# Half of the NSA output projection set between the last attention units of a hybrid decoder layer

## The chip, the core and the metric

The kernel runs on one core of a Trainium2 chip. The core has a matrix engine (TensorE, PE in the profile; its weight loads are listed as PEld), two elementwise engines that can read the accumulation banks (VectorE, DVE, and ScalarE, ACT), a third one, GpSimd (POOL), and SyncE (SP), which issues DMAs. Each engine works through its own queue in order and waits for the others by semaphores. The metric is the device time of one execution in microseconds (us); less is better.

## The reference, cut to what matters

```python
y_mla = mla_mixer(...)                    # 8 heads, causal softmax, width 512
y_nsa = nsa_mixer(...)                    # 8 heads in 2 groups, three gated branches, width 512
mixed = concatenate([rmsnorm(y_mla, g_out_mla), rmsnorm(y_nsa, g_out_nsa)], -1)
h = x + mixed @ w_o                       # (512, 1024) @ (1024, 1024)
a = relu(rmsnorm(h, g_mlp_norm) @ w_up)   # 1024 -> 4096
h = h + (a * a) @ w_down                  # 4096 -> 1024
out = rmsnorm(h, g_final)
```

There are 512 tokens, which the kernel treats as four tiles of 128 (t = 0 to 3), and everything is float32. Since `mixed` is two halves of 512 columns, `mixed @ w_o` is a sum of two products: an MLA part, and an NSA part that needs `y_nsa` of the same tokens.

## The kernel before

**Precision.** A float32 product is made of three passes on PE: each operand is split into a rounded high half and a low half (`split`, line 117: the high half by an ACT cast on line 111, the low half by a DVE subtraction on line 125), and `mm3` (lines 130 to 132) multiplies high by high, high by low and low by high.

**Attention.** Twenty-four units run one behind another in a software pipeline: eight MLA heads (s = 0 to 7), eight NSA units of the selected branch (s = 8 to 15), and eight NSA units that do the window and the compressed branch (s = 16 to 23: tokens t = 0, 1, 2, 3, two groups each). A unit writes scores into bank "A" (`s_ps`, lines 547 and 548), DVE masks them and takes the maximum (lines 552 and 556), ACT takes the exponential (line 560), PE transposes (`pt_ps`, line 585), ACT and DVE split, PE multiplies by the values (`ot_ps`, lines 596 and 597), ACT copies the result (`os`, line 619), PE folds it (`o_ps`, lines 621 and 623), DVE weighs it (`ow`, line 626) and POOL adds it into `yn` (line 629). A unit takes three rounds, so those of t = 0 are complete when s = 20 begins, those of t = 1 when s = 22 begins.

**Filling.** Between the steps of the units `fill(s)` takes steps of other work from two lanes. The second lane is `out_mla`: it loads and splits the MLA half of `w_o` and does the eight MLA products of the output projection (`out_proj`, lines 809 to 818: 12 matrix products of 128x512 into `wo_ps`, then one DVE addition into `xs` on line 818). The last of the eight (t = 3, columns 512 to 1023) is held back (`HELD`), until s is at least 22 (`FROM`). Right after it `load_wo` loads and splits the last quarter of `w_o` (the NSA half, columns 512 to 1023), on POOL (lines 798, 115 and 125).

**After the units.** `norm_y` squares and sums `yn` of all four tiles (ACT, line 783; `rsq` on DVE and POOL), `transpose_y` turns each tile on PE (`yt_ps`, line 805) and splits it into `yth` and `ytl`. The pools of the attention are released, so that the loads of `w_up` (`ur`, line 950, on the SP queue) can start. Then, for two column halves c and four tiles t, comes the NSA product of the projection (`out_proj(1, t, c, ...)` in bank "A", which has two buffers), the transposition of the sum (`ht_ps`, line 1080, bank "B"), a DVE scaling into `hs` (line 1082), and in between the splits that the MLP begins with: three tiles of `w_up` (`uw`), and token tiles `ttB11`, `ttT2`, `ttT1`, `ttB21` of which T2 needs all of `hs` for c = 0 and a DVE subtraction (line 1089) stands ahead of T1. The first MLP products (`up_ps`, line 990) use B11 (48 passes), then T2 (48), then B21.

**Order.** The queues are not in the order of the source: a scheduler places each engine's instructions when the program is built, so the diff doesn't tell where the work ends up.

Of the kernel before, what the change touches and what calls it, by code (L numbers as in the profile page):

```python
# [20 lines left out]
NT = T // P  # L21
# [5 lines left out]
RATES = (1.2, 1.2, 1.2, 1.0, 0.5, 1.4)  # L27
# [1 line left out]
ORDER = ((1, 2, 3, 0), (0, 1, 2, 3))  # L29
LAG = (0, 0)  # L30
CMPF = 0
HELD = 1
FROM = 22
SLACK = 8
WARM = 36
CSUM = "V"
QTE = "AAAA"
# [57 lines left out]
def layer(ctx, tc, x, xt, w_in, w_uq, w_ukv, w1k, w2k, w1v, w2v, w_o, w_up, w_down, g_final, consts, vecs, out):  # L95
    nc = tc.nc
# [74 lines left out]
    m = {}  # L171
# [39 lines left out]
    def steps(*gens):  # L211
        for g in gens:
            yield from g
# [562 lines left out]
    ny, ry = col(40, 8), col(48, 8)  # L776
    sh, r4 = col(56, 8), col(64)

    def norm_y(y, part):
        for t in range(NT):  # L780
            jy = m["wo"].tile([P, 4, P], F32, tag="wor", name="jy", bufs=2).rearrange("p a b -> p (a b)")
            at = 4 * part + t
            nc.scalar.activation(jy, y[:, t], AF.Square, accum_out=ny[:, at:at + 1])
            rsqrt_mean(ry[:, at:at + 1], ny[:, at:at + 1], 512)
# [37 lines left out]
    def out_mla():  # L822

        m["yth"] = m["wo"].tile([P, 4, 512], R32, name="yth")
        m["ytl"] = m["wo"].tile([P, 4, 512], R32, name="ytl")
        w = [load_wo(0, V_OM, 0, *WO_[0])]
        yield
        norm_y(ym, 0)
        yield
        for t in range(NT):  # L830
            sync.dma_start(m["xs"][:, t, :], x_t[:, t, :])
        for t in range(NT):
            transpose_y(ym, t, m["yth"][:, t], m["ytl"][:, t], "F")
            yield
        w.append(load_wo(0, V_OM, 1, *WO_[1]))
        todo = [(t, c) for c in range(2) for t in range(NT)]
        for n, (t, c) in enumerate(todo):
            if n == len(todo) - HELD:
                m["held"] = True
                yield  # L840
            yield from out_proj(0, t, c, w[c], m["yth"][:, t], m["ytl"][:, t], "F", 1)
            yield
            if (t, c) == (NT - 1, 0):
                m["won"] = [load_wo(1, V_ON, 0, *WO_[2])]
        m["won"].append(load_wo(1, V_ON, 1, *WO_[3]))

# [4 lines left out]
    lanes = [[(0, 6, RATES[0], chunk(C_CMP, "wc", post_c)), (0, 7, RATES[1], chunk(C_Q[0], "wq", post_q(0))),  # L853
              (0, 9, RATES[2], chunk(C_Q[1], "wq", post_q(1))), (6, 9, RATES[3], turn_q(0)), (10, 10, 1.0, turn_q(1)),
              *([] if CMPF else [(10, 17, RATES[4], steps(compressed(0), compressed(1)))])],
             [*([(10, 17, RATES[4], steps(compressed(0), compressed(1)))] if CMPF else []), (10, len(units) + 2, RATES[5], out_mla())]]
    due = [0.0, 0.0]
    live = []

    marks = []  # L860

    def fill(s):
        marks.append(next(i for i in reversed(nc.cur_bb.bb.instructions) if i.engine == mybir.EngineType.PE))
        for n, fills in enumerate(lanes):
            if fills and s >= fills[0][0]:
                due[n] += fills[0][2]
                while due[n] >= 1.0 and fills and s >= fills[0][0]:
                    due[n] -= 1.0
                    if n == 1 and m.get("held"):
                        if s < FROM:  # L870
                            break
                        with tc.issue_after(marks[-1 - SLACK]):
                            r = next(fills[0][3], "done")
                    else:
                        r = next(fills[0][3], "done")
                    if r == "done":
                        fills.pop(0)

    for s in range(len(units) + 2):
# [26 lines left out]
        for f in fills:  # L906
            whole(f[3])

    norm_y(yn, 1)
    w, yth, ytl = (m[n] for n in ("won", "yth", "ytl"))  # L910
    for t in range(NT):
        transpose_y(yn, t, yth[:, t], ytl[:, t], "B")
    wk2.release()
    wk.release()
# [157 lines left out]
    ready = []  # L1072
    for c in range(2):
        for t in range(NT):
            whole(out_proj(1, t, c, w[c], yth[:, t], ytl[:, t], "A"))
            cs = slice(512 * c, 512 * c + 512)
            b = bank("B", "ht_ps")
            for j in range(4):
# [181 lines left out]
```

## Time and profile before

| | |
|---|---|
| time, median of 3 runs | 652.48 us (652.03 to 653.15) |
| the profiled execution | 652.88 us, of which the span from first to last instruction is 651.0 us |
| PE busy | 635.2 us, 98% of the span |
| DVE, ACT, POOL busy | 429.9, 336.6, 240.0 us |
| clock of TensorE granted | 0.997 of full speed |

The stage that the change touches runs from 223 us (the first scores of the window units) over 276.9 us (the last matrix product of the attention) to 308.7 us (the first MLP product with T2). "Busy" of PE counts a modelled tail of each matrix product, so that neighbours overlap; the distance between two starts is the time that one costs.

### The profile page before, as it was taken

What the parts mean: (1) busy time and instruction counts of PE and PEld (TensorE: products, weight loads), DVE (VectorE), ACT (ScalarE), POOL (GpSimd) and SP (SyncE); (2) the same over time, 40 slices, a digit from 0 to 9 for tenths busy, and PEclk for the clock granted to TensorE, in tenths of its full rate; (3) what the DMA queues carried; (4) which work ended last, traced back from release to release, by engine and by line L of the source; (5) the groups of instructions that cost most, each with busy time, mean ns of one, the idle gap of its engine ahead of it and who ended that gap; (6) DMA issues with size and microseconds to landing.
All of it is one profiled execution on the core that took longest, in us unless ns stands there. A gap on an engine that the chain in (4) does not pass through costs nothing.

```text
span 651.0 us, 10981 instructions
## 1 busy us (share of the span) xinstructions
PE 635.2 (98%) x4092; PEld 571.5 (88%) x4092; DVE 429.9 (66%) x898; ACT 336.6 (52%) x702; POOL 240.0 (37%) x294
## 2 busy tenths in 40 slices
PE   7999999999999999999999999999999999999996
PEld 5989999998878888889998889988899988999885
DVE  5767577856788589768967435794259843497425
ACT  5567677857946478732884115541144521355213
POOL 3864402235783139613110225413154231344031
PEclk9999999999999999999999999999999999999998
DMA  6533210105322101063135313254122541124003
GB/s 193 154 99 82 68 50 17 33 2 195 99 78 88 33 2 33 1 216 108 46 116 163 98 33 98 88 171 131 33 81 63 181 140 55 63 68 147 15 2 129
DMA packets 47125, 56.53 MB, mean 87 GB/s; under 512 B 4320, under 2 KB 34784, under 8 KB 47072
## 3 DMA queue, kind: packets, MB, share of 16 engines
q1 hardware_dynamic: 46784, 55.57, 27.9%
q8 instruction: 32, 0.52, 0.3%
q10 hardware_dynamic: 288, 0.26, 0.1%
q14 instruction: 21, 0.17, 0.1%
HBM read 53.72 MB, written 2.10 MB: 86 GB/s over the span
## 4 chain that ended last, share of the span: by engine, by line
PE 86%; DVE 5%; DMA 3%; ACT 2%; POOL 2%; issue 1%; SPq 1%; POOLq 0%; ACTq 0%; DVEq 0%
PE up_ps L990 25%; PE dn_ps L131 9%; PE dn_ps L132 9%; PE dn_ps L130 9%; PE wo_ps L130 2%; PE wo_ps L132 2%; PE wo_ps L131 2%; PE pt_ps L585 2%; PE hid_ps L730 2%; PE s_ps L547 1%; PE pt_ps L692 1%; PE ot_ps L596 1%; PE wq_ps L132 1%; PE wq_ps L131 1%; PE wq_ps L130 1%; PE s_ps L548 1%
## 5 line engine op out<-in xcount | busy, mean ns | idle before, releaser
L130 PE MATMUL dn_ps<-dw,ah 128*128 128x512 f32 (+1 forms) x264 | 101.9, 386 | 0.0
L131 PE MATMUL dn_ps<-dw,ah 128*128 128x512 f32 (+1 forms) x264 | 101.9, 386 | 0.0
L132 PE MATMUL dn_ps<-dw,al 128*128 128x512 f32 (+1 forms) x264 | 101.7, 386 | 0.0
L990 PE MATMUL up_ps<-ttT,uw 128*128 128x256 f32 x720 | 89.5, 282 | 0.4
L990 PEld LDWEIGHTS up_ps<-ttT,uw 128*128 128x128 f32 x720 | 87.2, 189 | 1.0 <-ACT snap L1019 1.0
L990 PE MATMUL up_ps<-ttB,uw 128*128 128x256 f32 x648 | 82.0, 282 | 0.0
L990 PEld LDWEIGHTS up_ps<-ttB,uw 128*128 128x128 f32 x648 | 79.6, 189 | 0.5
L958 POOL TENSOR_TENSOR us<-us,ur 128x1024 f32<-128x1024 f32 x14 | 41.4, 2958 | 101.2 <-DVE uw L125 101.2
L958 POOL TENSOR_TENSOR us<-ur 128x1024 f32<-128x1024 f32 x14 | 35.3, 2530 | 99.8 <-DMA ur<-in_w_up 49.7
L125 DVE TENSOR_TENSOR uw<-us,uw 128x1024 fp32r<-128x1024 f32 x28 | 37.4, 1336 | 47.2 <-ACT uw L111 47.2
L125 DVE TENSOR_TENSOR dw<-dr,dw 128x1024 fp32r<-128x1024 f32 x32 | 43.8, 1368 | 35.3 <-ACT dw L111 35.3
L131 PEld LDWEIGHTS dn_ps<-dw,ah 128*128 128x128 f32 x264 | 49.6, 188 | 10.6
L130 PEld LDWEIGHTS dn_ps<-dw,ah 128*128 128x128 f32 x264 | 49.6, 188 | 10.5
L132 PEld LDWEIGHTS dn_ps<-dw,al 128*128 128x128 f32 x264 | 49.5, 188 | 10.6
L111 ACT CAST uw<-us 128x1024 fp32r<-128x1024 f32 x28 | 29.4, 1049 | 55.5 <-PE dn_ps L132 40.7
L125 DVE TENSOR_TENSOR uw<-ur,uw 128x1024 fp32r<-128x1024 f32 x25 | 39.5, 1582 | 25.6 <-ACT uw L111 25.6
L111 ACT CAST dw<-dr 128x1024 fp32r<-128x1024 f32 x32 | 33.2, 1048 | 38.0 <-PE dn_ps L132 21.5
L111 ACT CAST uw<-ur 128x1024 fp32r<-128x1024 f32 x25 | 26.2, 1049 | 29.9 <-PE dn_ps L132 26.7
L560 ACT ACTIVATE pr<-pr,mx 128x256 f32<-128x256 f32 (+3 forms) x64 | 36.0, 565 | 6.9 <-DVE mx L552 5.2
L125 DVE TENSOR_TENSOR pl<-pt_ps,ph 128x512 fp32r<-128x512 f32 (+3 forms) x60 | 34.2, 577 | 8.2 <-ACT ph L111 6.9
L111 ACT CAST ph<-pt_ps 128x512 fp32r<-128x512 f32 (+3 forms) x60 | 29.7, 499 | 15.5 <-PE pt_ps L585 5.4
L1156 DVE SCALAR_TENSOR_TENSOR xs<-dn_ps,small,xs 128x512 f32<-128x512 f32 (+1 forms) x33 | 23.0, 734 | 19.9 <-PE dn_ps L132 19.9
(326 smaller groups left out, 1533.5 us busy)
## 6 DMA issues: line engine op xcount, KB each, us to landing
ur<-in_w_up SPq DMA_DIRECT2D x32, 512.0 KB, 3.9
dr<-in_w_down SPq DMA_DIRECT2D x32, 512.0 KB, 3.8
wor<-in_w_o SPq DMA_DIRECT2D x16, 256.0 KB, 3.1
wqraw<-in_w_in SPq DMA_DIRECT2D x16, 128.0 KB, 2.2
xs<-in_x SPq DMA_DIRECT2D x4, 512.0 KB, 5.4
wmraw<-in_w_in SPq DMA_DIRECT2D x8, 208.0 KB, 4.3
xr<-in_xt SPq DMA_DIRECT2D x3, 512.0 KB, 3.8
out<-xs SPq DMA_DIRECT2D x6, 256.0 KB, 2.2
```

The source lines that it names most:

```text
L111: nc.scalar.copy(dst, src)
L125: (lo_eng or nc.vector).tensor_tensor(lo, src, hi.bitcast(F32), op=ALU.subtract)
L130: nc.tensor.matmul(o, a_hi, b_hi, start=first, stop=False)
L131: nc.tensor.matmul(o, a_hi, b_lo, start=False, stop=False)
L132: nc.tensor.matmul(o, a_lo, b_hi, start=False, stop=last)
L547: nc.tensor.matmul(S[:, :b - a], qs, ka[:, brg, a:b], start=True, stop=False)
L560: nc.scalar.activation(pr[:, :L], pr[:, :L], AF.Exp, bias=lim, scale=-1.0, accum_out=sums[:, 4 + h:5 + h])
L585: nc.tensor.transpose(b[:, h * P:(h + 1) * P], prs[h][:, j * P:(j + 1) * P], ident)
L730: nc.tensor.matmul(hp[0:96, 0:P], xx[:, 2 * i:2 * i + 16 * 95 + 1:16], w1[:, j, :], start=(i == 0), stop=(i == 15))
L958: add = lambda o, x, y: nc.gpsimd.tensor_tensor(o, x, y, op=ALU.add)
L990: nc.tensor.matmul(oj, v[:, x, k, s], t[:, y, k, :], start=first and j == 0 and k == 0 and n == 0, stop=k == 3 and n == 2, skip_group_chec ...
L1156: nc.vector.scalar_tensor_tensor(xs[:, t, cs], accs[t, a][:, a:b], r4[:, t:t + 1], xs[:, t, cs], op0=ALU.mult, op1=ALU.add)
```

## The change

The held product is not held any more: `out_mla` has to end by s = 20. A third lane takes two new pieces, `out_nsa(0)` from s = 20 and `out_nsa(1)` from s = 22, one step per `fill`. Such a piece does for one token tile what stood behind the units: the sum of squares, the four transpositions with their split, and the two products with their additions into `xs`, now in bank "W", which has one buffer. Behind the units only tiles 2 and 3 are left. Nothing is computed more or less than before. The lines of the changed kernel have numbers lower by two to four.

```diff
-HELD = 1
-FROM = 22
-SLACK = 8
+EARLY = 2
...
-    def norm_y(y, part):
-        for t in range(NT):
+    def norm_y(y, part, ts=range(NT)):
+        for t in ts:
...
-            if n == len(todo) - HELD:
-                m["held"] = True
-                yield
             yield from out_proj(0, t, c, w[c], m["yth"][:, t], m["ytl"][:, t], "F", 1)
...
+    def out_nsa(t):
+
+        norm_y(yn, 1, (t,))
+        yield
+        transpose_y(yn, t, m["yth"][:, t], m["ytl"][:, t], "W")
+        yield
+        for c in range(2):
+            yield from out_proj(1, t, c, m["won"][c], m["yth"][:, t], m["ytl"][:, t], "W", 1)
+            yield
...
-             [*([(10, 17, RATES[4], steps(compressed(0), compressed(1)))] if CMPF else []), (10, len(units) + 2, RATES[5], out_mla())]]
-    due = [0.0, 0.0]
+             [*([(10, 17, RATES[4], steps(compressed(0), compressed(1)))] if CMPF else []), (10, 20, RATES[5], out_mla())],
+             [(20 + 2 * t, len(units) + 2, 1.0, out_nsa(t)) for t in range(EARLY)]]
+    due = [0.0, 0.0, 0.0]
...
-                    if n == 1 and m.get("held"):
-                        if s < FROM:
-                            break
-                        with tc.issue_after(marks[-1 - SLACK]):
-                            r = next(fills[0][3], "done")
-                    else:
-                        r = next(fills[0][3], "done")
-                    if r == "done":
+                    if next(fills[0][3], "done") == "done":
...
-    norm_y(yn, 1)
+    norm_y(yn, 1, range(EARLY, NT))
...
-    for t in range(NT):
+    for t in range(EARLY, NT):
         transpose_y(yn, t, yth[:, t], ytl[:, t], "B")
...
-            whole(out_proj(1, t, c, w[c], yth[:, t], ytl[:, t], "A"))
+            if t >= EARLY:
+                whole(out_proj(1, t, c, w[c], yth[:, t], ytl[:, t], "A"))
```

What this makes of the queues is seen at three places. The first is PE's queue where the window units begin, behind the last product of the compression (`hid_ps`); `wo_ps` with `yth` and `ytl` is the projection, `s_ps` with 128x160 are the first scores of a window unit. Before:

```order
L730 MATMUL hid_ps<-w_3311,xw 96x128 x4
L547 MATMUL s_ps<-ka,qt_2367 128x160
L548 MATMUL s_ps<-kb,qt_2367 128x160
L585 MATMUL pt_ps<-cst,pr 128x128 x2
L642 MATMUL o_ps<-cst,os 128x128 x4
```

After:

```order
L728 MATMUL hid_ps<-w_3311,xw 96x128 x4
L128 MATMUL wo_ps<-woh,yth 128x512
L129 MATMUL wo_ps<-wol,yth 128x512
L130 MATMUL wo_ps<-woh,ytl 128x512
L128 MATMUL wo_ps<-woh,yth 128x512
L640 MATMUL o_ps<-cst,os 128x128
```

The 12 matrix products of the MLA piece that was held now stand in one block ahead of the first window scores; before, they stood 66 rows further on, between the scores of t = 2.

The second place is PE's queue behind the last scores of t = 2 (128x416). Before, the value products and transpositions of the next units follow at once:

```order
L547 MATMUL s_ps<-ka,qt_2487 128x416
L548 MATMUL s_ps<-kb,qt_2487 128x416
L577 MATMUL pct_ps<-cst,pc 128x128
L585 MATMUL pt_ps<-cst,pr 128x128 x4
L597 MATMUL ot_ps<-pl,vc 128x512
L596 MATMUL ot_ps<-ph,vc 128x512
```

After:

```order
L595 MATMUL ot_ps<-pl,vc 128x512
L575 MATMUL pct_ps<-cst,pc 128x128
L583 MATMUL pt_ps<-cst,pr 128x128 x4
L619 MATMUL o_ps<-vbd_76,pct 128x256
L128 MATMUL wo_ps<-woh,yth 128x512
L129 MATMUL wo_ps<-wol,yth 128x512
L130 MATMUL wo_ps<-woh,ytl 128x512
```

Here begins the first of four blocks of 12 such products (t = 0 and c = 0); the others follow after about 10, 24 and 10 rows of attention, and the last ends ahead of the last six pairs of scores of t = 3.

The third place is behind the attention, where DVE prepares the MLP. `ow` is the last weighing of the attention, `hs` the scaled sum, `tt` the token tiles (T2 comes first of the two `ttT`), `uw` the split `w_up`. Before:

```order
L818 SCALAR_TENSOR_TENSOR xs<-wo_ps,small,xs 128x512
L1082 TENSOR_TENSOR hs<-ht_ps,vec 128x4x128
L125 TENSOR_TENSOR uw<-ur,uw 128x1024
L125 TENSOR_TENSOR ttB_4258<-hs,ttB_4258 128x1024
L818 SCALAR_TENSOR_TENSOR xs<-wo_ps,small,xs 128x512
L1082 TENSOR_TENSOR hs<-ht_ps,vec 128x4x128
L1089 TENSOR_TENSOR hs<-hs 128x4x256
L818 SCALAR_TENSOR_TENSOR xs<-wo_ps,small,xs 128x512
L125 TENSOR_TENSOR ttT_4262<-hs,ttT_4262 128x1024
```

After:

```order
L123 TENSOR_TENSOR uw<-ur,uw 128x1024
L816 SCALAR_TENSOR_TENSOR xs<-wo_ps,small,xs 128x512
L1079 TENSOR_TENSOR hs<-ht_ps,vec 128x4x128
L123 TENSOR_TENSOR uw<-ur,uw 128x1024
L816 SCALAR_TENSOR_TENSOR xs<-wo_ps,small,xs 128x512
L123 TENSOR_TENSOR uw<-ur,uw 128x1024
L816 SCALAR_TENSOR_TENSOR xs<-wo_ps,small,xs 128x512
L1079 TENSOR_TENSOR hs<-ht_ps,vec 128x4x128 x2
L1086 TENSOR_TENSOR hs<-hs 128x4x256
L123 TENSOR_TENSOR ttT_4318<-hs,ttT_4318 128x1024
```

The low half of T2 keeps its place behind the three `uw` and the subtraction, and on PE half of the products that stood ahead of its use are gone.

## Rows read from the trace of the kernel before

**Rows 1.** The page: the chain that ended last, by engine.

```profile
PE 86%; DVE 5%; DMA 3%; ACT 2%; POOL 2%; issue 1%; SPq 1%; POOLq 0%; ACTq 0%; DVEq 0%
```

**Rows 2.** By stretch: its us; busy us of PE, PEld, DVE, ACT, POOL; clock, DMA.

```profile
223.30:241.10 17.80, 17.24 (x116) 14.51 (x116) 16.70 (x104) 14.43 (x50) 5.20 (x8) 1.00 0.00 1
241.10:249.90 8.80, 8.80 (x52) 7.36 (x51) 7.01 (x31) 5.97 (x19) 6.80 (x10) 1.00 0.17 48
249.90:262.00 12.10, 11.96 (x80) 10.18 (x79) 11.74 (x58) 10.84 (x30) 12.00 (x16) 1.00 0.03 11
262.00:276.90 14.90, 14.85 (x101) 12.37 (x100) 11.30 (x34) 10.69 (x25) 8.40 (x11) 1.00 0.01 1
276.90:308.70 31.80, 31.80 (x185) 27.56 (x185) 24.91 (x29) 9.22 (x11) 7.79 (x5) 1.00 0.53 166
```

**Rows 3.** Waits of PE's weight loads, 249.9 to 262: first and last of four.

```profile
PEld o_ps L623 <- ACT os L619: 0.3, 1, 0.3
...
PEld s_ps L547 <- PE pct_ps L577: 0.2, 1, 0.2
```

**Rows 4.** Timeline of PE: start, us, engine, line; the held block, first and last.

```profile
223.28 0.32 PE L547 MATMUL s_ps<-ka,qt 128*128 128x160 f32 x1
...
241.10 0.39 PE L130 MATMUL wo_ps<-woh,yth 128*128 128x512 f32 x1
...
243.84 0.39 PE L132 MATMUL wo_ps<-woh,ytl 128*128 128x512 f32 x1
```

**Rows 5.** Timeline of DVE around the first window scores and behind the held block.

```profile
223.75 0.29 DVE L552 CUSTOM_DVE_ANT_0 pr<-s_ps,cst 128x128 f32<-128x128 f32 x1 [1.04 <-PE s_ps L548]
...
244.27 0.75 DVE L818 SCALAR_TENSOR_TENSOR xs<-wo_ps,small,xs 128x512 f32<-128x512 f32 x1 [1.53 <-PE wo_ps L132]
244.94 0.55 DVE L552 CUSTOM_DVE_ANT_0 pr<-s_ps,cst 128x384 f32<-128x384 f32 x1
```

**Rows 6.** Timeline of POOL (splitting the last quarter of w_o) and of DVE beside it.

```profile
242.34 0.17 DVE L518 SCALAR_TENSOR_TENSOR rg<-sums,sg 128x8 f32<-128x8 f32 x1
...
245.50 2.71 POOL L125 TENSOR_TENSOR wol<-wor,woh 128x512 fp32r<-128x512 f32 x2
...
255.07 0.66 DVE L518 SCALAR_TENSOR_TENSOR rg<-sums,sg 128x8 f32<-128x8 f32 x1
```

**Rows 7.** Timeline of PE behind the attention: transposes of tiles 2 and 3, T2.

```profile
276.95 0.61 PE L805 MATMUL yt_ps<-cst,yn 128*128 128x128 f32 x4
...
282.70 0.38 PE L805 MATMUL yt_ps<-cst,yn 128*128 128x128 f32 x2
...
308.69 5.85 PE L990 MATMUL up_ps<-ttT,uw 128*128 128x256 f32 x48
```

**Rows 8.** Timeline of ACT and of POOL behind the attention.

```profile
277.92 1.56 POOL L629 TENSOR_TENSOR yn<-yn,ow 128x256 f32<-128x256 f32 x2 [3.51 <-DVE ow L626]
...
283.12 0.59 ACT L111 CAST yth<-yt_ps 128x512 fp32r<-128x512 f32 x1 [2.88 <-PE yt_ps L805]
```

**Rows 9.** Timeline of DVE behind the attention.

```profile
286.96 1.21 DVE L125 TENSOR_TENSOR uw<-ur,uw 128x1024 fp32r<-128x1024 f32 x1
288.10 0.68 DVE L1082 TENSOR_TENSOR hs<-ht_ps,vec 128x512 f32<-128x512 f32 x1
...
294.73 3.00 DVE L1089 TENSOR_TENSOR hs<-hs 128x1024 f32<-128x1024 f32 x1
298.32 3.90 DVE L125 TENSOR_TENSOR ttT<-hs,ttT 128x1024 fp32r<-128x1024 f32 x2
```

**Rows 10.** The tile ur, 270 to 330: POOL's additions (ns min/median/max, starts), landing.

```profile
L958 POOL TENSOR_TENSOR us<-ur x2: 2392/2892/3392, 294.2 to 296.6; 128x1024 f32<-128x1024 f32 x2
...
DMA to landing us min/median/max: 4.0/4.7/9.1
```

More of the change, by code (lines that the diff above doesn't have):

```diff
@@ L855, in layer @@
               *([] if CMPF else [(10, 17, RATES[4], steps(compressed(0), compressed(1)))])],
-             [*([(10, 17, RATES[4], steps(compressed(0), compressed(1)))] if CMPF else []), (10, len(units) + 2, RATES[5], out_mla())]]
-    due = [0.0, 0.0]
+             [*([(10, 17, RATES[4], steps(compressed(0), compressed(1)))] if CMPF else []), (10, 20, RATES[5], out_mla())],
+             [(20 + 2 * t, len(units) + 2, 1.0, out_nsa(t)) for t in range(EARLY)]]
+    due = [0.0, 0.0, 0.0]
     live = []
-    marks = []
     def fill(s):
-        marks.append(next(i for i in reversed(nc.cur_bb.bb.instructions) if i.engine == mybir.EngineType.PE))
         for n, fills in enumerate(lanes):
```

## The prediction

> **What bounds the kernel now.** I read the chain of work that ended last first: PE carries 86% of it [rows 1]. So time can only be won where PE waits, and what the change adds to another engine costs nothing until PE has to wait for it. The table of stretches then parts the stage in five [rows 2]. DVE is busy 16.70 of 17.80 us in the first, where the window units begin, 7.01 of 8.80 in the second, 11.74 of 12.10 in the third, 11.30 of 14.90 in the fourth: up to 262 us DVE is as full as PE, and in the first and third it sets the pace. In the fifth, behind the attention, PE is full (31.80 of 31.80) and DVE has 24.91. Last come the waits of PE's weight loads, the only place where a filler can win: in the third stretch they are four, 1.1 us together [rows 3]. That is the prize. It is small because the stage is already packed.
>
> **The change, part by part.** All sums stand against the profiled execution (652.88 us, 0.40 above the median); I add the difference to the median, 652.48.
>
> *Blocks that move.* From the first to the last of the 12 products of the held block 2.74 us pass, with one value product of the same width among them: 12 steps of 0.23 us [rows 4]. Four blocks of 12 are 11.0 us. They leave the fifth stretch and enter the third: nothing by themselves. Their four loads of weights are no new ones, and no DMA on SP's queue is held up by them: the loads of w_up still wait for the last addition into yn.
>
> *The held MLA block* goes from 241.1 to 223.3, ahead of the first window scores. There DVE is waiting for those scores already (1.04 us of idle before 223.75 [rows 5]), so all 2.75 us delay it; 0.15 more for the addition, so +2.9. In its old place DVE sat idle for 1.53 us before the addition and spent 0.67 on it (244.27 to 244.94) [rows 5]: taking it away gives 2.2 back there, because DVE sets the pace. Net **+0.7**, between 0 (if the early block hides 0.7 of DVE's work) and +1.3 (if only the 1.53 comes back).
>
> *DVE's part of the pieces.* Two low halves (0.6 each) and four additions (0.67 each) enter. The low half of tile 0 falls into the second stretch, where DVE has no room: **+0.6**. The rest falls beside the blocks in the third, where PE then has 12.1 - 1.1 + 11 + 0.4 = 22.4 us of work and DVE 11.7 + 3.3 = 15.0: hidden; its cover is the blocks themselves.
>
> *POOL.* The last quarter of w_o is split earlier, because the product that held its buffers is gone earlier: some 10 us of POOL work (two of its subtractions take 2.71 [rows 6]) leave the second and third stretches and stand in the first, ahead of the subtractions of the window units' maxima (line 564). A DVE instruction of the same shape takes 0.17 beside an idle POOL and 0.66 beside this work [rows 6]. The first stretch has the more of such small instructions; I take +0.5 there and -0.3 in the second: **+0.2**, between -0.5 and +1.5 (the upper end if the maxima wait too).
>
> *Filling* wins the waits of the third stretch, 1.1 [rows 3]; I take **-1.0**, and 0.3 more in the fourth, where DVE starts without a backlog: **-0.3**. Bounds -1.8 and 0.
>
> *Behind the attention.* Let 0 be the moment when PE is done with the last fold, 276.95 before [rows 7]. Before, T2 is used at +31.7 [rows 7]; its low half ends by 302.2, less the 1.2 us of the T1 split behind it, +24.1 [rows 9]: 7.6 us of cover. After, PE has 48 products less ahead of T2. Its walk along the new order, with prices from rows 4 and 7 (four transpositions 0.36, a pass of 256 columns 5.7 / 48 = 0.12): transposition 0.36, ten products 2.3, transposition 0.36: at +3.0 it turns the last half of tile 3, whose yn POOL finished at +2.5 [rows 8]. The next product needs its high half, which before was there 1.0 us after the transposition began (282.70 to 283.71) [rows 7, 8]; PE has only 0.24 of work: **+0.8**, a wait that was covered before. Then 14 products, a transposition, 10 products: +9.9, end of the second product of the projection; 15 passes with B11, 12 products, 7 passes, eight transpositions in two groups, and the rest of the 48 passes between two more groups: +19.8. From above, the old 31.7 less 48 products (11.0), six transpositions for yt that now stand earlier (0.5) and four for ht that stand later (0.4), with the 0.8, is +20.6; I take this, since the sum of prices leaves out the small losses between unlike instructions.
>
> DVE meanwhile: the addition of that second product can't run before +10.2, and stands ahead of the second uw (low halves 1.14 from start to start [rows 9]). Addition 0.67, hs 0.6, uw 1.14: +12.6. That frees the buffer of a load that POOL needs, landing some 4.2 later, +16.8 (the shortest took 4.0 [rows 10]). DVE: addition, third uw, the addition of the third product (PE ends it at +14.5), two hs (after PE's transposition at +15.6): +17.1. Now the subtraction on line 1089. Before, it began while POOL was adding (294.25), took 3.00 us where its like take 1.2, and ended 1.1 after POOL's first addition of 2.4 us, at 296.6 [rows 9, 10]; T2's low half then met the second one, at 298.32, and the two T splits took 3.90. So with POOL starting at +16.8 the subtraction ends at 16.8 + 2.4 + 1.1 = +20.3, and T2 at **+21.5**: PE waits 21.5 - 20.6 = **+0.9**. Bounds: none, if DVE gets in ahead of POOL (17.1 + 2 x 1.14 = 19.4), and +3.2, if POOL's second addition gets in ahead of T2 (16.8 + 2.4 + 1.1 + 2.4 + 1.1 = 23.8). I take the middle, because the order of the two starts, 16.8 and 17.1, hangs on the same addition. [...]
>
> Behind T2, B21 and the other tiles follow with their cover: DVE ends B21 some 4 us later than T2, PE needs it 5.7 us later.
>
> *Sum*: 0.7 + 0.6 + 0.2 - 1.0 - 0.3 + 0.8 + 0.9 = **+1.9**: 652.48 + 1.9 = **654.4**.
>
> **Rivals.**
> 1. *DVE gets ahead of POOL*, T2 is in time: +1.0, **653.5**, no difference. For it: the margin is 0.3 us in a walk of 17. Against it: both hang on the same addition.
> 2. *Faster: the blocks really fill.* PE's waits of the third and fourth stretches go whole, 1.1 and 1.4 at the most, the early MLA block costs nothing because DVE catches up, tile 3 and T2 are in time: -2.5 + 0.6 + 0.2 = -1.7, **650.8**. It decides if DVE keeps less than one unit of backlog at the first block. For it: DVE is at 15.0 of 22.4 us there. Against: four small waits can't be met by blocks of 12 [rows 3]. [...]
> 3. *The blocks stall the units.* The pieces don't come piece by piece: on PE each stands as 12 products in a row. The addition behind each waits on DVE ahead of a low half that PE's next value product needs, as it did at 244.27 [rows 5]. By the order PE has about 0.95 us of other work, DVE needs 0.25 + 0.67 + 0.2 + 0.6 = 1.7: 0.75 a block, four times 3.0 more: **657.4**. Against: the first and third have more attention behind them.
>
> **How the numbers follow.** Forecast 0.42, rival 1 0.30, rival 2 0.13, rival 3 0.15. A measurement of this kernel can tell some 0.2%, 1.3 us, from no change. Slower is the forecast and rival 3, 0.57; the same is rival 1, 0.30; faster is rival 2, 0.13. The range: the low end takes in rival 1 with its low bounds (held block 0, POOL -0.5: 651.5), the high end rival 3 as it stands, 657.4; left out are most of rival 2 and what lies above rival 3.
>
> **What would show it.** In the changed profile: DVE's first window maximum near 226 to 227 instead of 223.75, and no idle of 1.5 us in the second stretch; the last fold some 11 to 12 us later than 276.9; then T2's first pass 21 to 22.5 us after that fold (31.7 before), the subtraction taking about 3 us beside a POOL addition, and a wait of PE's weight load for DVE ttT. I am wrong on the last term if that wait is missing; on the filling if the last fold comes less than 10.5 us later; and rival 3 holds if ot_ps waits for pl behind each block.

## The result, and the profile after

The changed kernel takes 662.45 us (median of 4 runs, 661.24 to 665.05), the kernel before 652.62 beside it (652.03 to 653.15): a ratio of 1.0158, with a 95% interval of 1.0141 to 1.0174. It is slower, as forecast, but by 9.8 us where 1.9 were forecast, and outside the range. The profiled execution of after is the one of 661.24 us; its span is 659.4.

First the chain that ended last, by engine, from the page of after. It answers [rows 1]: PE has gone from 86% to 82%, DVE from 5% to 7%, ACT from 2% to 4%.

```profile
PE 82%; DVE 7%; ACT 4%; POOL 3%; issue 2%; DMA 2%; SPq 1%; POOLq 0%; ACTq 0%; DVEq 0%
```

Then the stretches, as in [rows 2] (us; busy us of PE, PEld, DVE, ACT, POOL; clock, DMA). The last two are cut where the last fold ends now, 293.85.

```profile
223.30:241.10 17.80, 15.24 (x85) 13.31 (x84) 14.60 (x70) 8.47 (x30) 10.20 (x13) 0.81 0.10 30
241.10:249.90 8.80, 8.20 (x53) 6.99 (x52) 7.72 (x43) 7.66 (x26) 5.02 (x7) 1.00 0.01 2
249.90:262.00 12.10, 12.06 (x74) 10.33 (x73) 11.12 (x47) 8.82 (x25) 6.83 (x9) 1.00 0.00 0
262.00:293.85 31.85, 30.25 (x185) 25.26 (x184) 20.11 (x70) 17.68 (x42) 10.12 (x13) 1.00 0.01 2
293.85:322.30 28.45, 26.16 (x178) 23.71 (x178) 22.82 (x25) 11.10 (x13) 7.72 (x5) 1.00 0.59 185
```

The first stretch has changed most. Of the same 17.80 us PE is busy 15.24 instead of 17.24, POOL 10.20 instead of 5.20, and the granted clock, 1.00 before, is 0.81 on the average. The third is full, as forecast (12.06 of 12.10).

Times from the start can't be set against each other as they are. Up to this product PE has the same order in both kernels; it starts at 218.65 before and at 217.48 after:

```profile
218.65 0.40 PE L596 MATMUL ot_ps<-ph,vc 128*128 128x512 f32 x1
217.48 0.40 PE L594 MATMUL ot_ps<-ph,vc 128*128 128x512 f32 x1
```

This execution of after was 1.2 us ahead there, 1.0 of it at 66 us already, far from the change. An execution of another kernel with the order of before on PE, DVE and ACT (e13_stand_alone, below) is 1.0 ahead at the same product, so the lead belongs to the execution. Counted from that product, and set against the work that moved (four blocks, 11.0, and the transpositions for them, 0.5), the time went here:

| us | before | after | moved | lost |
|---|---|---|---|---|
| from the common product to the end of the last fold | 58.30 | 76.37 | +11.5 | 6.6 |
| from there to the products behind T2 | 37.43 | 28.49 | -11.5 | 2.6 |
| from there to the end | 336.67 | 337.06 | 0 | 0.4 |

Together 9.5. The two profiled executions differ by 8.4 (661.24 - 652.88) because of the lead of 1.2; the medians differ by 9.8.

Now the place of the loss: the timeline of after from 225 to 232 us, PE, then DVE, then POOL (start, us, engine, line; in brackets the idle time before and what ended it).

```profile
228.12 0.44 PE L594 MATMUL ot_ps<-ph,vc 128*128 128x512 f32 x1
230.61 0.53 PE L595 MATMUL ot_ps<-pl,vc 128*128 128x512 f32 x1 [2.06 <-DVE pl L123]
...
227.41 0.89 DVE L742 TENSOR_TENSOR gw<-z 128x64 f32<-128x64 f32 x1
228.33 1.16 DVE L743 TENSOR_SCALAR gw<-gw 128x64 f32<-128x64 f32 x1
...
229.88 0.68 DVE L123 TENSOR_TENSOR pl<-pt_ps,ph 128x512 fp32r<-128x512 f32 x1
...
225.77 1.20 POOL L113 TENSOR_SCALAR woh<-wor 128x512 fp32r<-128x512 f32 x2
226.94 2.50 POOL L123 TENSOR_TENSOR wol<-wor,woh 128x512 fp32r<-128x512 f32 x2
```

PE stands for 2.06 us before a value product, because DVE is late with `pl`. DVE is late because two instructions of the gelu (`gw`, 64 elements a partition) take 0.89 and 1.16 us where they take 0.22 and 0.20 beside an idle POOL (e3_pool_later, below). They run beside the two subtractions with which POOL splits the last quarter of `w_o`: these end at 228.2 and 229.4, and each `gw` ends 0.1 us behind one of them.

What follows the stand is in the same view as above, cut finer:

```profile
229.00:230.00 1.00, 0.00 (x0) 0.00 (x0) 1.00 (x4) 0.01 (x1) 0.44 (x1) 1.00 0.65 195
230.00:231.00 1.00, 0.39 (x1) 0.20 (x2) 1.00 (x6) 0.45 (x2) 0.00 (x0) 0.98 0.66 199
231.00:237.00 6.00, 6.00 (x28) 5.74 (x28) 4.77 (x30) 3.80 (x16) 4.94 (x8) 0.50 0.07 23
237.00:238.00 1.00, 1.00 (x4) 0.50 (x3) 0.99 (x4) 0.54 (x2) 0.88 (x1) 0.61 0.00 0
```

Behind the stand the granted clock is 0.50 for 6 us and 0.61 in one more, 6.8 us at half clock by these rows. PE is busy all that time. Products of 512 columns start every 0.43 us at this clock instead of 0.23 (e13_stand_alone, below), so by an estimate half of the 6.8 us is lost: 3.0 + 0.4 = 3.4 us. With the stand of 2.06 and two small waits after it (0.5 for `vbd`, 0.4 for `cm`) that is 6.4, close to the 6.6 lost up to the last fold. The match is rough: PE waits for 1.6 us more on the way to the fold, and time at half clock is not lost whole (see e5_adds_behind_t1 and e10_pl_first).

Behind the attention, PE, DVE and POOL again, answering [rows 7 to 9]:

```profile
298.10 0.50 PE L128 MATMUL wo_ps<-woh,yth 128*128 128x512 f32 x1 [0.68 <-ACT yth L109]
...
314.33 0.40 PE L986 MATMUL up_ps<-ttT,uw 128*128 128x256 f32 x2
316.34 2.52 PE L986 MATMUL up_ps<-ttT,uw 128*128 128x256 f32 x19 [1.61 <-DVE ttT L123]
...
311.34 1.63 DVE L1086 TENSOR_TENSOR hs<-hs 128x1024 f32<-128x1024 f32 x1
312.89 3.39 DVE L123 TENSOR_TENSOR ttT<-hs,ttT 128x1024 fp32r<-128x1024 f32 x1
...
309.51 5.69 POOL L954 TENSOR_TENSOR us<-ur 128x1024 f32<-128x1024 f32 x2 [11.27 <-issue]
```

Both waits that were forecast are there: 0.68 for `yth` of the last tile, and 1.61 for the low half of T2. The first passes of T2 begin 20.5 us after the last fold without a wait; the third is the one that waits.

### The profile page after: what moved, and what is told of

It is laid out like the page before. It is cut to its first block, busy times and chain, and to the rows that moved or that the text cites. A ratio compares the mean times of both kernels' runs of the same rounds, so it can differ in the third digit from the quotient of the medians.

```text
span 659.4 us, 10977 instructions
## 1 busy us (share of the span) xinstructions
PE 638.5 (97%) x4092; PEld 575.9 (87%) x4092; DVE 434.2 (66%) x898; ACT 336.9 (51%) x702; POOL 242.8 (37%) x294
## 4 chain that ended last, share of the span: by engine, by line
PE 82%; DVE 7%; ACT 4%; POOL 3%; issue 2%; DMA 2%; SPq 1%; POOLq 0%; ACTq 0%; DVEq 0%
PE up_ps L986 21%; PE dn_ps L130 9%; PE dn_ps L129 9%; PE dn_ps L128 9%; PE wo_ps L128 2%; PE wo_ps L130 2%; PE wo_ps L129 2%; PE pt_ps L583 2%; PE hid_ps L728 2%; PE s_ps L545 1%; PE pt_ps L690 1%; PE ot_ps L594 1%; PE ot_ps L595 1%; PE s_ps L546 1%; PE wq_ps L129 1%
## 5 line engine op out<-in xcount | busy, mean ns | idle before, releaser
L954 POOL TENSOR_TENSOR us<-us,ur 128x1024 f32<-128x1024 f32 x14 | 43.0, 3068 | 95.7 <-DVE uw L123 95.7
L123 DVE TENSOR_TENSOR uw<-ur,uw 128x1024 fp32r<-128x1024 f32 x25 | 39.7, 1587 | 26.6 <-ACT uw L109 26.6
```

What stands on the lines that cost most here:

```text
L123: (lo_eng or nc.vector).tensor_tensor(lo, src, hi.bitcast(F32), op=ALU.subtract)
L954: add = lambda o, x, y: nc.gpsimd.tensor_tensor(o, x, y, op=ALU.add)
```

## The experiments

Theory A, read from this trace: POOL's split, which now stands at 226 to 238 us, makes DVE late; PE stands; the clock falls. Theory B: the pieces themselves, or the early MLA block, cost it. All times are medians; "before" is 652.5 to 653.1 in these runs.

**The pieces left out** (they run behind the attention as before; block and split stay early):

```diff
-EARLY = 2
+EARLY = 0
```

> The changed kernel without its four NSA pieces (EARLY = 0): the held MLA block still stands at its new, early place and the last quarter of w_o is still split early on POOL. Theory A (the early split on POOL holds DVE, PE then stands for about 2 us for pl at the first window units, and the granted clock falls to the lower level behind it): both show here too, at about 226 to 238 us, and the time is 5 to 6 us above the kernel before, 657.5 to 658.5. Theory B (the pieces themselves cost it, between the units): no such loss, at most the 1 us of the moved block, 652.5 to 653.5.

658.61 us, 1.0088 of before (1.0064 to 1.0111). PE stands for 2.07 us up to 231.09, in front of the same product, and the clock is 0.50 behind it, for at least 13.1 us by these rows:

```profile
230.00:231.00 1.00, 0.00 (x0) 0.00 (x0) 1.00 (x4) 0.26 (x1) 0.00 (x0) 0.93 0.75 242
231.00:244.00 13.00, 12.56 (x49) 11.12 (x50) 9.84 (x58) 6.50 (x24) 6.82 (x10) 0.50 0.06 20
```

Behind the last fold this execution takes as long as before (37.41 us to the products behind T2), so what it loses lies ahead of the fold. The pieces are not the main cause: 5.5 of the 9.8 stay without them.

**POOL's split later**, behind POOL work of unit 20; the block stays early, the pieces stay:

```diff
-        m["won"].append(load_wo(1, V_ON, 1, *WO_[3]))
...
     def out_nsa(t):
...
+        if t == 0:
+            last = next(i for i in reversed(nc.cur_bb.bb.instructions) if i.engine == mybir.EngineType.Pool)
+            with tc.issue_after(last):
+                m["won"].append(load_wo(1, V_ON, 1, *WO_[3]))
```

> The changed kernel with the load and the split of the last quarter of w_o put behind POOL work of unit 20, so that POOL is nearly idle between 225 and 232 us as in the kernel before; the MLA block stays early, the pieces stay. Theory A (POOL's early split): the gelu's small DVE instructions take about 0.2 us again instead of 0.9 to 1.2, PE does not stand for 2 us before its value product, the clock stays 1.00, and the time is 5 to 6 us below the changed kernel, 656.5 to 657.5. Rival (the early MLA block alone makes DVE late): the wait for pl at about 230 us stays over 1 us, and the time stays within 1 us of 662.4.

655.96 us, 1.0044 (1.0029 to 1.0059): 6.5 us of the 9.8 are gone, a little more than expected. Its timeline, DVE and PE, and one stretch:

```profile
227.73 0.22 DVE L742 TENSOR_TENSOR gw<-z 128x64 f32<-128x64 f32 x1
227.98 0.20 DVE L743 TENSOR_SCALAR gw<-gw 128x64 f32<-128x64 f32 x1
...
229.38 0.51 PE L595 MATMUL ot_ps<-pl,vc 128*128 128x512 f32 x1 [0.51 <-DVE pl L123]
```

```profile
231.00:237.00 6.00, 6.00 (x43) 5.03 (x43) 5.61 (x38) 5.08 (x19) 0.40 (x1) 1.00 0.01 1
```

`gw` takes 0.2 us again, PE waits 0.51 instead of 2.06, and in the six microseconds from 231 PE issues 43 products where the changed kernel issued 28. From the common product (217.80 here) to the end of the last fold (288.32) it is 12.2 us longer than before, for 11.5 of moved work: with the split out of the way, block, pieces and filling together cost 0.7 in the attention. Another 3.0 lie behind it (2.6 up to the products behind T2, 0.5 further on).

**PE kept busy in the stand.** A first try put nine more products two units too late (they ran at 238.2, when the clock, 0.50 from 232 to 238, was about to rise: 0.82 from 238 to 239):

```diff
+                if (br, i, g) == (1, 0, 0):
...
+                    for n in range(9):
+                        last = nc.tensor.matmul(idle, vc[:, 4 * j + brg, :], ph, start=True, stop=True)
```

> The changed kernel with nine more products (128x512, into a bank that nobody reads) on PE ahead of the product that waits for pl at about 228 us: some 2 us of PE work in place of the stand. Theory (the clock falls because PE stood): the granted clock stays 1.00 behind it, the 3.3 us of half clock are gone, 659 us. Rival (the clock falls at that time whatever PE does, or the 2 us of stand alone are the whole loss): the clock falls all the same, or nothing is won, 662 to 664.5 us.

660.21 us. The stand (2.07) and the half clock behind it are as in the changed kernel, so this run tells nothing of the clock. The second try put them where PE stands:

```diff
+                if (br, i, g) == (0, 0, 1):
+                    for n in range(9):
+                        nc.tensor.matmul(ot, vc[:, 4 * j + brg, :], ph, start=True, stop=True)
                 nc.tensor.matmul(ot, vc[:, 4 * j + brg, :], ph, start=(j == 0), stop=False)
```

> The changed kernel with nine more products (128x512, into the bank that the next product starts anew) on PE just ahead of the value product that waited for pl at 228 to 230.6 us; e4_busy_pe had them two units later, where PE did not stand. POOL's split and DVE's lateness are left as they are. Theory (the granted clock falls because PE stood before): PE's stand shrinks from 2.1 us to under 0.5, the clock stays 1.00 from 231 to 238, and the time is 2 to 3.5 us below the changed kernel, 659 to 660.5 us. Rival (the clock falls there for another reason): the clock is 0.50 for some 6 us all the same and the time 662 to 664.

664.59 us, 1.0181 (1.0166 to 1.0196): the time was missed, the clock was not. Its stretches, and from its timeline PE and DVE:

```profile
229.00:232.00 3.00, 2.98 (x15) 2.20 (x14) 2.97 (x10) 0.69 (x5) 1.62 (x2) 1.00 0.34 100
...
236.00:237.00 1.00, 0.07 (x1) 0.00 (x0) 0.96 (x4) 0.00 (x0) 0.92 (x3) 1.00 0.00 0
...
238.00:239.00 1.00, 0.00 (x0) 0.00 (x0) 0.93 (x6) 0.00 (x0) 0.10 (x1) 0.85 0.00 0
239.00:244.00 5.00, 4.70 (x18) 4.47 (x19) 2.88 (x20) 2.76 (x10) 0.40 (x1) 0.50 0.00 0
```

```profile
239.30 0.58 PE L545 MATMUL s_ps<-ka,qt 128*128 128x288 f32 x1 [3.23 <-DVE cm L554]
...
234.94 4.00 DVE L774 COPY vbd<-kc 32x64 f32<-32x64 f32 x8
```

With PE full from 229 to 232 the clock stays 1.00. But the order of the rows behind has changed, and DVE now meets the rest of POOL's split with eight small copies, 4.00 us instead of 1.6 in the kernel before. PE stands for 3.23 us, and behind that stand the clock is 0.50. So the half clock follows the stand.

**A stand alone.** In the kernel before, one product of the down projection waits for a chain of POOL subtractions, and what PE has behind it is kept behind it; nothing else is changed, and the orders of PE, DVE and ACT are the same:

```diff
...
+                    for _ in range(3):
+                        nc.gpsimd.tensor_tensor(junk, xs[:, 0, 0:512], xs[:, 0, 0:512], op=ALU.subtract)
+                    nc.gpsimd.tensor_tensor(ws[0][:, 0, 0:1], ws[0][:, 0, 0:1].bitcast(F32), junk[:, 0:1], op=ALU.add)
                 mm3(accs[t, a][:, a:b], ah[:, s], al[:, s], v[:, 0, j, a:b], v[:, 1, j, a:b],
...
```

> The kernel before with nothing but one stand of PE in the down projection (second quarter, first product of c = 1), far from POOL's split and from the window units: that product waits for a chain of three POOL subtractions (128x512, 1.2 to 1.3 us each) that begins with the addition of the first token tile of c = 0; the orders of PE, DVE and ACT are unchanged. The stand should be some 2.5 to 3 us. Theory (a stand of this length brings the granted clock down behind it, whatever caused it): the clock is 0.50 for some 6 to 7 us behind the stand, which costs 3.3 us more, 658 to 659 us. Rival (a stand costs its own length, and the clock fell in the changed kernel for another reason): the clock stays 1.00, 655 to 655.6 us.

657.91 us, 1.0082 (1.0063 to 1.0102). PE's timeline and the stretches of the profiled execution (656.67 us):

```profile
455.08 0.80 PE L130 MATMUL dn_ps<-dw,ah 128*128 128x512 f32 x1 [3.29 <-POOL dw L1156]
```

```profile
452.00:454.00 2.00, 0.00 (x0) 0.00 (x0) 1.63 (x2) 0.92 (x1) 1.84 (x3) 1.00 0.25 88
454.00:455.00 1.00, 0.00 (x0) 0.00 (x0) 0.98 (x1) 0.00 (x0) 1.00 (x1) 0.79 0.00 0
455.00:458.00 3.00, 2.92 (x7) 2.34 (x8) 0.00 (x0) 0.00 (x0) 0.03 (x1) 0.50 0.00 0
458.00:460.00 2.00, 2.00 (x11) 1.61 (x10) 0.00 (x0) 0.00 (x0) 0.00 (x0) 1.00 0.00 0
```

In a stage with nothing of the change in it, the clock goes to 0.50 behind a stand. The rest of this execution, from the products behind T2 to the last, is 4.76 us longer than before: 3.29 of stand and 1.5 of half clock, which lasted 3.4 us here against 6.8 in the changed kernel. The median is 5.4 above before, and this execution, which was 1.0 ahead before the stand, the shortest of six; what the others lost is in no trace.

**POOL's work alone**, in the kernel before: two scalings and two subtractions of the split's shapes, at the same place on POOL.

```diff
...
+            if m["apart"] == 12:
...
+                with tc.issue_after(add.ins):
+                    for n in range(2):
+                        nc.gpsimd.tensor_scalar(junk, masks, 1.0, 1.0, op0=ALU.mult, op1=ALU.mult)
+                    for n in range(2):
+                        nc.gpsimd.tensor_tensor(junk, masks, masks, op=ALU.subtract)
```

> The kernel before with nothing but four more POOL instructions (two scalings, two subtractions of 128x512, the shapes of the split, into a tile nobody reads) behind the addition into yn at 225.3 us; MLA block and NSA products stay where they were, the orders of PE and DVE are the same. Theory (POOL's work there is the whole cause): DVE's gelu instructions beside it take 0.9 to 1.2 us instead of 0.2, PE stands 1 to 2 us for pl, the clock falls to 0.50 for some 6 us, and the time is 4 to 6 us above the kernel before, 656.5 to 658.5. Rival (it needs the early MLA block too, which brings DVE behind): PE's waits at 226 to 232 stay under 0.7 us, the clock stays 1.00, 652.5 to 653.5.

654.26 us, 1.0028 (1.0016 to 1.0040): between the two. DVE, PE and POOL in its timeline:

```profile
229.79 1.02 DVE L754 TENSOR_SCALAR gw<-gw 128x64 f32<-128x64 f32 x1
...
231.28 0.31 PE L547 MATMUL s_ps<-ka,qt 128*128 128x160 f32 x1 [0.35 <-DVE cm L556]
...
229.72 2.16 POOL L655 TENSOR_TENSOR junk<-cst 128x512 f32<-128x512 f32 x2
```

`gw` is held as in the changed kernel (1.02 us, where it takes 0.18 in the kernel before), with no load of `w_o` beside it, so it is POOL's work that holds it. But `pl` stood ahead of it on DVE, PE's waits stay under 0.6 and the clock at 1.00. So POOL's work costs 1.6 here, and not 6. Three things differ from the changed kernel: DVE's order, the MLA block, which stands late here, and the amount, 3.5 us of POOL work (1.32 + 2.16) where the split has 8.9.

**DVE's order alone**: in the changed kernel, `pl` put ahead of `gw` again (the gelu's end may come one unit later for it).

```diff
-        nc.vector.tensor_tensor(w_, z, z, op=ALU.mult)
+        while kv == 1 and "pl" not in m:
+            yield
+        if kv == 1:
+            with tc.issue_after(m["pl"]):
+                nc.vector.tensor_tensor(w_, z, z, op=ALU.mult)
...
```

> The changed kernel with one order on DVE turned back to that of the kernel before: the low half pl of the last unit ahead of the window (tile 0, second group) stands ahead of the gelu's small instructions gw instead of behind them (they are made to follow it). POOL's early split and the early MLA block stay. Theory (it takes both: POOL's split, which slows gw, and a DVE order that puts pl behind gw; e7_pool_in_before had only the first and lost 1.6 us): PE's stand of 2.1 us before that product goes to under 0.5, and if no other stand of 2 us comes up later, the clock stays 1.00 and the time is 655.5 to 658. Rival (POOL's rest of the split makes PE stand at another place, as in e6_busy_here at 236 us): a new stand of over 2 us within 10 us, the clock falls behind that one, 660 to 664.

660.88 us (659.0 to 666.44), 1.0143 (1.0102 to 1.0183). Its stretches and one row of PE, in an execution of 659.52 us:

```profile
230.00:231.00 1.00, 0.55 (x4) 0.56 (x5) 0.96 (x10) 0.78 (x4) 0.30 (x1) 1.00 0.46 166
231.00:237.00 6.00, 5.10 (x31) 3.60 (x30) 5.89 (x38) 4.36 (x19) 5.52 (x8) 1.00 0.08 30
```

```profile
230.45 0.31 PE L545 MATMUL s_ps<-ka,qt 128*128 128x160 f32 x1 [1.44 <-DVE cm L554]
```

The wait for `pl` is gone, and PE waits at the next places instead: 1.44 for the maxima, then five times 0.2 to 0.8. So the order of `pl` is not the cause; DVE's delay by POOL is, wherever it comes out. The clock stays 1.00 in this execution, behind a stand of 1.44; the two longest of the four runs (662.24 and 666.44) have mean clocks of 0.987 and 0.985 against 0.996 here, so it probably fell in them, but no trace shows where. From the common product to the last fold it is 1.9 us less than in the changed kernel and 3.9 more than in e3_pool_later: that is the price of the split without the half clock. Why e7_pool_in_before paid only 1.4 by the same count, whether for the smaller amount or for the late MLA block, no run separates.

**POOL's first additions of `w_up` behind the split of T1**, by a copy of one column on DVE:

```diff
         s3 = mh.tile([P, 1024], F32, tag="us", name="us", bufs=2)
+        if g == 1:
+            nc.vector.tensor_copy(s[:, 0:1], tt["T1"][:, 1, 0, 0:1].bitcast(F32))
         add(s, a[1, 0], a[1, 1])
```

> The changed kernel with one tiny DVE copy (128x1) behind the split of T1, on which POOL's first two additions of w_up (us) wait: the orders of PE and POOL are unchanged, DVE's has this one row more. Theory (POOL's additions hold DVE's subtraction and the split of T2): the subtraction takes 1.2 us, T2 is split some 2 to 3 us earlier, the wait of the weight load for DVE ttT (1.8 us) goes, 660.6 us. Rival (T2 is late because its inputs are late, or the sums us are then late for the first Strassen unit): no gain, 662 to 664 us.

661.20 us, 1.0123 (1.0106 to 1.0140). DVE, POOL and PE:

```profile
314.03 1.22 DVE L1088 TENSOR_TENSOR hs<-hs 128x1024 f32<-128x1024 f32 x1
315.17 1.22 DVE L123 TENSOR_TENSOR ttT<-hs,ttT 128x1024 fp32r<-128x1024 f32 x1
...
310.74 2.39 POOL L954 TENSOR_TENSOR us<-ur 128x1024 f32<-128x1024 f32 x1 [9.81 <-DMA ur<-in_w_up]
320.13 2.40 POOL L954 TENSOR_TENSOR us<-ur 128x1024 f32<-128x1024 f32 x1 [7.00 <-DVE us L958]
...
317.02 2.66 PE L988 MATMUL up_ps<-ttT,uw 128*128 128x256 f32 x21
```

Subtraction and split take 1.22 each, PE begins T2 20.5 us after the last fold and goes through without the wait, and from the last fold to the products behind T2 it is 26.6 us instead of 28.5. The additions, late now, give 0.6 back further on, so the median gains 1.2, though the runs of the two kernels overlap.

Up to the last fold all four engines have the order of the changed kernel here, and the stand is 2.06 us again. But the half clock behind it lasted at least 12.6 us by these rows instead of 6.8:

```profile
232.00:233.00 1.00, 0.92 (x6) 0.88 (x6) 1.00 (x11) 1.00 (x7) 0.92 (x2) 0.67 0.08 29
233.00:245.00 12.00, 11.65 (x47) 10.22 (x46) 8.41 (x44) 5.92 (x21) 6.37 (x9) 0.50 0.00 1
```

The last fold came 2.4 us later for it, from the common product on. So 5.8 us more at half clock, at the least, cost 2.4 in this place: less than half their length, since some of it takes the place of waits (0.6 us of waits that the changed kernel has at 238 to 242 us are gone here).

**The parts put together otherwise.** Four kernels ask what the rest is worth, and whether a version beats both. e8_both has the split later and the additions behind T1. e12_one_tile is the same with `EARLY = 1`. e9_block_only has the split later and `EARLY = 0`, that is, only the early block. e11_block_held is the kernel before with its held block in place, plus the pieces (from s = 22) and the additions behind T1:

```diff
+            if fills and s >= fills[0][0] and not (n == 2 and len(m.get("won", ())) < 2):
...
+             [(22 + t, len(units) + 2, 1.0, out_nsa(t)) for t in range(EARLY)]]
```

> The changed kernel with both edits: the last quarter of w_o split later on POOL (as e3_pool_later) and POOL's first additions of w_up behind the split of T1 (as e5_adds_behind_t1). If the two losses are separate, they add: 655.96 less the 1.85 us that the stretch from the last fold to the products of B21 won in e5_adds_behind_t1, 654.1 us. If the wait for T2 only moves to the next operand, 655.5 to 656. To beat the kernel before it would have to be under 651.5; nothing so far gives that.

> As e8_both (early MLA block, late split of the last quarter of w_o, additions behind T1) with the pieces of one tile of tokens only (EARLY = 1, two blocks). If the pieces fill little, it lies between the kernel before and e8_both's 655.0, near 654; if they are what pays for the early block (e9_block_only without any: 656.65), it lies between these two, 655.5 to 656.

> The kernel before with the one difference that the held MLA block runs early, ahead of the first window scores: no NSA pieces (EARLY = 0), and the last quarter of w_o split late, as in e3_pool_later. The prediction's term for the moved block: 0.7 us slower (0 to 1.3), 653.2 to 653.6. Rival (the block is free, since the last fold of e3_pool_later came 0.2 us early after 11.5 us of moved work): 652.3 to 652.9.

> The pieces alone: the kernel before with its held MLA block at its old place (and so POOL's split of the last quarter of w_o at its old time), the four NSA pieces behind it, and POOL's first additions of w_up behind the split of T1 as in e5_adds_behind_t1. By the prediction's terms: the pieces fill 1.3 us and cost 0.6 on DVE; behind the attention the stretch from the last fold to the products of B21 is 0.8 us worse than by count (as in e8_both), and 0.9 comes on later: 652.7 - 0.7 + 1.7 = 653.7. Rival (the pieces fill more, as e3_pool_later against e9_block_only makes it look, where the last fold came 4.4 us earlier than by count): 650 to 652, ahead of the kernel before. Rival (they stall the units, 0.75 each): 656 to 657.

| kernel | us | ratio (95%) |
|---|---|---|
| e8_both | 655.03 | 1.0038 (1.0026 to 1.0050) |
| e12_one_tile | 654.38 | 1.0028 (1.0018 to 1.0037) |
| e9_block_only | 656.65 | 1.0060 (1.0048 to 1.0073) |
| e11_block_held | 656.27 | 1.0056 (1.0042 to 1.0070) |

The two repairs nearly add (654.1 expected). None of the four beats the kernel before. e9_block_only missed both expectations: its last fold ends 4.2 us later than before, and more than half of the loss lies where the late split now runs without pieces beside it, in the stretches of [rows 2] (the last one to its own last fold):

```profile
241.10:249.90 8.80, 8.48 (x45) 5.77 (x44) 8.73 (x47) 7.65 (x27) 8.80 (x12) 1.00 0.09 32
249.90:262.00 12.10, 11.21 (x76) 9.64 (x75) 11.00 (x42) 9.66 (x25) 12.03 (x15) 1.00 0.08 23
262.00:281.17 19.17, 18.02 (x120) 15.18 (x119) 14.28 (x52) 13.46 (x34) 9.24 (x13) 1.00 0.00 1
```

PE is idle for 0.3, 0.9 and 1.2 us there, against 0.0, 0.1 and 0.1 before. Since the planner set a new order for the whole window branch, this doesn't price the block by itself. e11_block_held landed on the number of the third case, but not by stalled units. Up to its last fold PE does 58 products, six transpositions for `yt` and four for `ht` more than before, 14.2 us by count, in 13.4 us: there the pieces won 0.8, as its expectation had it (-0.7). The loss lies behind the fold, 5.3 by the same count up to the products behind T2: three waits in a row (0.9 for `hs`, 0.4 for `yn`, 0.8 for `yth`), and behind them 6.8 us at half clock:

```profile
290.00:293.00 3.00, 1.57 (x11) 0.85 (x9) 1.98 (x3) 0.60 (x2) 1.45 (x2) 1.00 0.00 0
293.00:299.00 6.00, 5.36 (x13) 4.20 (x14) 3.30 (x4) 3.54 (x6) 0.55 (x1) 0.50 0.91 288
```

## Why the prediction was wrong in size

The step that failed is **the term for POOL**, +0.2 with an upper bound of 1.5. It measured 6.5 (662.45 against 655.96), 5.9 of it up to the last fold in the two profiled executions. The prediction saw the work move (10 us of it), saw where to, and had the row of a small DVE instruction that takes 0.66 instead of 0.17 [rows 6]. It then failed in three ways:
- It priced one small instruction and not the queue. The first stretch has DVE 16.70 of 17.80 us busy [rows 2], so each delay there goes to whoever waits for DVE. Walking DVE's rows in the new order from 225 us on, it would have met three `gw`, then `pl`, then eight copies, and PE's product behind `pl`.
- The row behind the bounds had 0.5 us of delay; here one instruction lost 1.0 (1.16 against 0.20) and ended 0.1 us behind a POOL subtraction of 1.25 us. The bound of 1.5 is about what two fifths of this work cost in the kernel before (1.6, e7_pool_in_before).
- It took waits to cost their own length. Behind a stand PE ran for 6.8 us at half clock. Gross that is 3.4 us of work by the estimate from the product starts; the execution without it (e10_pl_first) was only 1.9 shorter up to the fold, since waits came in its place. No row of the kernel before shows a stand of 2 us in this stage, so this had no row to be read from, but the width of the range didn't allow for it.

The other steps, one by one:
- **Moved blocks**, nothing by themselves: right. Without the early split 11.5 of moved work made the attention 12.2 longer; the 0.7 belongs to the next item.
- **Held block and DVE's part of the pieces**, +0.7 and +0.6, **filling**, -1.3: their sum, 0.0, came out as +0.7 in e3_pool_later, within the bounds. Pieces and filling without the early block were forecast at -0.7 and came out as -0.8 in e11_block_held. That leaves some 1.5 for the early block instead of 0.7, an estimate from two kernels whose orders differ; e9_block_only, meant to measure it, didn't. The early block did delay DVE more than forecast: the first maximum came 4.0 later than before, counted from the common product, and not 2.9. That it stood at 226.56, inside the forecast 226 to 227, is luck: this execution was 1.2 ahead. The third stretch did fill, but at the end of the attention of the changed kernel PE waits four times, 1.5 us together.
- **`yth` of tile 3**, +0.8: right, 0.68.
- **T2**, +0.9 (0 to 3.2): the mechanism is right, the term too small. It measured 1.61 in the row and 1.9 in e5_adds_behind_t1. POOL began at +15.7 instead of +16.8, so its first addition was nearly over when DVE came to the subtraction (1.63 instead of the forecast 3), and the second one held the split of T2 (3.39, where it takes 1.22 in e5_adds_behind_t1). That is the case that the prediction had kept for its upper end. That a DVE start ahead of POOL would have cost nothing, as the lower bound and the first rival have it, was an estimate that no run shows: POOL began first here (309.51 against 311.34) and in e3_pool_later (303.95 against 305.82). The walk of PE along the new order held: T2's first pass at +20.5, forecast +20.6. The sign that was named, T2's first pass at 21 to 22.5, failed, because the high half was there and PE ran two passes before it needed the low half.
- **Rivals.** None came. T2 was not in time (1); block, pieces and filling didn't win on balance, since the attention took 0.7 more than the moved work even without the early split (2); behind the blocks no `ot_ps` waits for `pl` (3), the only such waits being at 289.27 (0.45, for POOL) and in the first stretch. What came was not among the rivals: a stand far ahead of the pieces, made by an engine that carried 2% of the chain before [rows 1].

With the measured terms the sum comes out: 5.9 for the split, 0.7 for the rest of the attention, 0.7 for `yth`, 1.9 for T2, and 0.4 towards the end are 9.6, against 9.5 in the profiled executions and 9.8 in the medians. What the 0.4 is, no run shows.

## What to carry to other kernels

When an edit frees a buffer early, ask which helper's work starts with it, and walk the queue of the engine whose instructions the rows show to be longer beside that helper (here DVE beside POOL: 0.89 and 1.16 us against 0.22 and 0.20), row by row, up to the first instruction that the bound engine waits for; the sum of the delays there is the price, not the delay of one instruction. A gap on PE can cost more than its length (3.29 us of stand and 1.5 of half clock in e13_stand_alone), so a range should have room for one such gap where a DVE-paced stretch gets new work beside it. In a kernel whose order a planner sets, one part undone gives a new order everywhere behind it: compare between fixed points, from the last instruction that both have in the same order to one such as the last fold, and not from the start, where one execution can lead another by 1 us for no reason of the change; and trust most those runs whose orders stay the same.

## What the hardware showed

The granted clock behind a gap of PE, in the traces of this case:

| kernel | PE's gap, us | clock behind it |
|---|---|---|
| changed | 2.06 | 0.50 for 6.8 us |
| e1_no_pieces | 2.07 | 0.50 for at least 13.1 us |
| e5_adds_behind_t1 | 2.06 | 0.50 for at least 12.6 us |
| e6_busy_here | 3.23 | 0.50 from 239 to past 244 |
| e13_stand_alone | 3.29 | 0.50 for 3.4 us |
| e11_block_held | 0.9, 0.4 and 0.8, from 290.5 to 293.6 | 0.50 from 293, for 6.8 us |
| changed, near its start | 1.12 and 0.23, from 6.1 to 7.9 | 1.00 up to 9, then 0.50 for 3.4 us |
| changed, ahead of T2 (316.34) | 1.61 | 1.00 |
| e10_pl_first | 1.44 | 1.00 |
| e3_pool_later | 0.51 | 1.00 |

At 0.50 products of 512 columns start every 0.43 us instead of 0.23 (e13_stand_alone). In these rows the clock fell only behind idle time of PE, and it stayed low while PE was busy again (6.00 of 6.00 us from 231 on in the changed kernel). How long the low level lasts differs from case to case, from 3.4 us to at least 13.1, even behind the same stand in the same order (6.8 in the changed kernel, at least 12.6 in e5_adds_behind_t1), and what decides it these runs don't show. The times of kernels with such a gap also lie further apart: 661.24 to 665.05 for the changed kernel, 656.67 to 659.65 for e13_stand_alone, against 652.03 to 653.15 for the kernel before. The longer executions of the changed kernel have the lower mean clock: 0.991 and 0.993 for 661.24 and 661.66 us, 0.988 and 0.985 for 663.24 and 665.05.
